# State-space layer with in-place decay matrices, and an order of TensorE's work that is tied to the projections

## The chip, the core and the metric

The kernel runs on one core of a Trainium2 chip. A core has five engines with a queue of instructions each: TensorE (matrix products, PE in the profile, its weight loads PEld), VectorE (DVE), ScalarE (ACT), GpSimd (POOL) and SyncE (SP, which only issues DMAs here). Each engine works through its queue in order and waits on semaphores. The metric is the device time of one execution in microseconds (us); the kernel before was timed three times.

## The reference

The reference is a trunk of two layers over a sequence of 512 tokens of width 1024. Each layer is a half-step SwiGLU feed-forward, a token mixer, and a second half-step feed-forward; every one is modulated, gated, added to the residual and normalised. The mixer of layer 0 is a bidirectional state-space layer, that of layer 1 a differential attention.

```python
for i in range(DEPTH):                      # 2
    y = swiglu(modulate(x, mods[:, 0]), ...)
    x = layer_norm(ALPHA * x + 0.5 * gate(0) * y, ...)
    u = modulate(x, mods[:, 1])
    y = mamba2_bidir(u, ...) if i % 2 == 0 else diff_attention(u, ...)
    x = layer_norm(ALPHA * x + gate(1) * y, ...)
    y = swiglu(modulate(x, mods[:, 2]), ...)
    x = layer_norm(ALPHA * x + 0.5 * gate(2) * y, ...)
```

In the state-space layer, `proj = u @ w_in` gives for each of 4 groups the inputs `xs` (8 heads of 64), `B`, `C` and the gate `z`; `xs`, `B` and `C` go through a convolution of width 3 and a SiLU. Each head then needs, for both directions, `y = (CB * L) X + C states`, where `L` is the matrix of decays, the exponential of differences of cumulated sums. The result is gated by SiLU(z), normalised per group and projected by `w_out`. In the attention, a head takes the difference of two softmaxes, multiplies it with the values, normalises, and the 8 heads are projected by `w_out`.

## The kernel before

Activations lie transposed: 8 tiles of 128 features by 512 tokens (`res`, the residual, and `u`, the input of a stage). Weights come as 128 x 1024 tiles of float32 (`load`, line 93, a DMA by SyncE) and are split into a high part on ScalarE (line 123) and a low part on VectorE (line 124), so that a product of float32 accuracy is three matmuls (`mm3`, line 162; every projection matmul stands on line 166). A projection (`proj`, line 172) of eight 128-blocks and 512 tokens is 24 matmuls of 512 columns.

The program is written as one stream of operations over tiles from rings of buffers (`bufs=`). Before the run a scheduler lays out each engine's queue from that text: an operation that stands earlier has precedence, but a later one is put ahead where the scheduler's own model of the durations says that the earlier one isn't ready. So TensorE's order is not that of the text, and it is fixed once the kernel runs. `tc.add_manual_dep(..., NOSYNC, ...)` ties one instruction behind another in that layout, without a semaphore.

**State-space layer (`ssm`, line 589).** For each group g of 4, in eight half steps (`for s in range(8)`, line 865): at each even s two heads (a pair) are opened by `ssd_head` (line 757). It loads the pair's rows `rw` and `ch` from a scratch in device memory (lines 761 and 763), and GpSimd writes the masks (line 778). For each half c of the sequence, `ssd_mats` (line 783) makes for each head a tile `E` with four exponentials on ScalarE (lines 786 to 789), an addition on GpSimd (line 792) and a multiplication with `cb` on VectorE (line 793); `ssd_out` (line 796) multiplies on TensorE (line 803, `mid` banks). `rw` has a ring of 2 tiles, `E` of 5. Between the half steps stand the projections of the next group (`units_bc`, `units_x`, `units_z`: up to 10) and the output projections of the group before (`outp`, 4 steps). When the projections are done, the SiLUs run in one batch (`silu`, line 711) and `prepare` (line 716) makes the next group's `B` transposed, `cb`, the transposed inputs `xt` and the states: 20 transposes and 8 products on TensorE (lines 721, 729, 742, 751), with copies on ScalarE between them. `gated_norm` (line 805) of the group before stands behind half steps 0 and 2.

**Layer norm (`LN`, line 262).** When the first of the eight residual tiles is complete, `start` (line 269) makes a first guess of the mean and subtracts it from all eight tiles on VectorE (line 278). Each tile that follows gets its addition (`add_res`, line 371, VectorE line 372), then sums and squares (`feed`, line 282). `finish` (line 408) does the last tiles in two halves of the tokens, with `stats` (line 294) and `normalize` behind each.

**End of the attention.** For the last head, h == 7, the output projection of heads 0 to 3 to the first four residual tiles stands between the score steps (`outp`, line 1023). The rest (`merged_units`, line 424) follows behind the last head: heads 4 to 7 to tiles 0 to 3, then all heads to tiles 4 to 7 in halves. The last head's chain is: scores, softmax, transposes (line 987), values (line 998), mean square (line 1004), root (line 247), broadcast (line 253).

## Time and profile before

| | us |
|---|---|
| three timed runs | 2180.67, 2181.95, 2177.81 |
| median | 2180.67 |
| profiled execution | 2176.88 |
| of it the span, first to last instruction | 2174.8 |
| state-space layer, about | 365 to 775 of the span |
| attention, about | 1500 to 1775 of the span |

The page shows busy time of each engine over the span, and the mean granted clock of TensorE is 0.993 of full speed. A stretch in the profile is a window of the span; its row gives the busy time and, in brackets, the number of instructions in it. Where the instructions of one line alone are asked for, the row counts only these. Among the busiest operations beside the matmuls are the weight splits:

```profile
L123 ACT ACTIVATE wh<-raw 128x1024 fp32r<-128x1024 f32 (+1 forms) x210 | 212.8, 1021 | 277.5 <-PE acc L166 95.4
...
L124 DVE TENSOR_TENSOR wl<-raw,wh 128x1024 fp32r<-128x1024 f32 (+1 forms) x210 | 248.4, 1185 | 46.7 <-ACT wh L123 45.4
L471 DVE TENSOR_TENSOR wl<-raw,wh 128x1024 fp32r<-128x1024 f32 x198 | 240.8, 1219 | 38.9 <-ACT wh L470 38.1
```

In such a row stand the line, the engine, what is written and read, the number, then the total busy time in us and the mean of one in ns, then the engine's idle time ahead of them and what ended it.

### The profile page before, as it was taken

Reading aid. Unit: us, or ns where it says so; the run is one execution under the profiler, and the core shown is the slowest. Engines: PE = TensorE matmul, PEld = TensorE weight load, DVE = VectorE, ACT = ScalarE, POOL = GpSimd, SP = SyncE. Lnnn points to the kernel's source line nnn. Section 1 sums busy time; section 2 is a strip of 40 time slices with the busy share of each in tenths; the row PEclk is TensorE's granted clock in tenths of the full one; section 3 lists DMA queues with packets and bytes.
Section 4 is the critical chain, followed back from the end, with each engine's and each line's share of the span. In section 5 each row is a group of like instructions: output and inputs, shape, how many; then the busy total and the mean of one; then the engine's idle time right before and its main releaser. Section 6 shows DMA issues by size and latency. Waiting matters only on the chain.

```text
span 2174.8 us, 34198 instructions
## 1 busy us (share of the span) xinstructions
PE 2119.9 (97%) x13206; PEld 1859.7 (86%) x13206; DVE 1775.3 (82%) x3086; ACT 1092.4 (50%) x1828; POOL 154.2 (7%) x258
## 2 busy tenths in 40 slices
PE   7999999999999989999999999999999989999997
PEld 6889899866777778999999989899888869989897
DVE  6979899556766689989889998987877879858697
ACT  4424354767655546434356534343866637424353
POOL 0000000045232300000000000000111100000000
PEclk9999999999999999999999999999999989999999
DMA  9863644464535423646443273723322212323231
GB/s 324 302 212 121 219 138 149 123 183 137 158 123 155 121 68 126 214 144 198 159 132 105 97 261 96 254 94 111 98 80 79 76 59 78 127 69 117 84 110 39
DMA packets 90082, 301.18 MB, mean 138 GB/s; under 512 B 10048, under 2 KB 13504, under 8 KB 89920
## 3 DMA queue, kind: packets, MB, share of 16 engines
q1 hardware_dynamic: 88384, 294.81, 41.7%
q0 software_dynamic: 1536, 4.20, 0.9%
q8 instruction: 103, 1.69, 0.3%
q14 instruction: 59, 0.48, 0.1%
HBM read 289.53 MB, written 5.24 MB: 136 GB/s over the span
## 4 chain that ended last, share of the span: by engine, by line
PE 59%; DVE 3%; issue 2%; ACT 2%; POOL 1%; DMA 0%; POOLq 0%; ACTq 0%; DVEq 0%; SPq 0%
PE acc L166 47%; PE mid L166 9%; PE mid L965 1%; PE ln L166 1%; PE ln L987 0%; DVE resid L278 0%; DMA raw<-in_wgu 0%; DVE resid L320 0%; PE ln L253 0%; PE ln L302 0%; ACT p L975 0%; POOL E L792 0%; ACT wh L123 0%; PE ln L1004 0%; DVE p L968 0%
## 5 line engine op out<-in xcount | busy, mean ns | idle before, releaser
L166 PE MATMUL acc<-hi,wh 128*128 128x256 f32 (+1 forms) x1592 | 533.1, 336 | 9.2 <-DVE resid L372 7.1
L166 PE MATMUL acc<-hi,wl 128*128 128x256 f32 (+1 forms) x1592 | 532.6, 335 | 0.0
L166 PE MATMUL acc<-lo,wh 128*128 128x256 f32 (+1 forms) x1592 | 532.1, 335 | 0.1
L166 PE MATMUL acc<-uh,wh 128*128 128x256 f32 (+1 forms) x1160 | 391.2, 338 | 0.0
L166 PE MATMUL acc<-ul,wh 128*128 128x256 f32 (+1 forms) x1160 | 389.6, 336 | 0.0
L166 PE MATMUL acc<-uh,wl 128*128 128x256 f32 (+1 forms) x1160 | 388.9, 336 | 0.0
L123 ACT ACTIVATE wh<-raw 128x1024 fp32r<-128x1024 f32 (+1 forms) x210 | 212.8, 1021 | 277.5 <-PE acc L166 95.4
L166 PEld LDWEIGHTS acc<-hi,wh 128*128 128x128 f32 x1592 | 302.9, 190 | 45.5 <-DVE resid L372 6.6
L470 ACT ACTIVATE wh<-raw 128x1024 fp32r<-128x1024 f32 x198 | 209.1, 1059 | 259.4 <-DVE raw L480 129.1
L166 PEld LDWEIGHTS acc<-lo,wh 128*128 128x128 f32 x1592 | 302.9, 190 | 31.0 <-DVE lo L154 1.3
L166 PEld LDWEIGHTS acc<-hi,wl 128*128 128x128 f32 x1592 | 303.0, 190 | 30.3 <-issue 0.5
L124 DVE TENSOR_TENSOR wl<-raw,wh 128x1024 fp32r<-128x1024 f32 (+1 forms) x210 | 248.4, 1185 | 46.7 <-ACT wh L123 45.4
L471 DVE TENSOR_TENSOR wl<-raw,wh 128x1024 fp32r<-128x1024 f32 x198 | 240.8, 1219 | 38.9 <-ACT wh L470 38.1
L166 PEld LDWEIGHTS acc<-uh,wh 128*128 128x128 f32 x1160 | 219.0, 189 | 28.6 <-issue 6.2
L166 PEld LDWEIGHTS acc<-ul,wh 128*128 128x128 f32 x1160 | 219.3, 189 | 25.1 <-issue 3.2
L166 PEld LDWEIGHTS acc<-uh,wl 128*128 128x128 f32 x1160 | 219.2, 189 | 23.7 <-issue 2.4
L480 DVE TENSOR_TENSOR raw<-raw 128x512 f32<-128x512 f32 x264 | 181.3, 688 | 5.0
L184 DVE SCALAR_TENSOR_TENSOR raw<-raw,cond 128x1024 f32<-128x1024 f32 x144 | 174.1, 1218 | 9.9 <-DMA raw<-in_adaw 9.7
L372 DVE SCALAR_TENSOR_TENSOR resid<-acc,gv,resid 128x512 f32<-128x512 f32 (+1 forms) x166 | 109.4, 663 | 58.8 <-PE acc L166 58.4
L316 POOL TENSOR_TENSOR rr<-vr,mhalf 128x2 f32<-128x2 f32 x12 | 8.4, 698 | 1527.6 <-DVE vr L312 1527.6
L166 PE MATMUL mid<-uh,wh 128*128 128x256 f32 (+2 forms) x332 | 99.8, 302 | 0.0
L166 PE MATMUL mid<-uh,wl 128*128 128x256 f32 (+2 forms) x332 | 99.3, 299 | 0.0
(266 smaller groups left out, 3920.7 us busy)
## 6 DMA issues: line engine op xcount, KB each, us to landing
raw<-in_wgu SPq DMA_DIRECT2D x176, 512.0 KB, 4.2
raw<-in_adaw SPq DMA_DIRECT2D x144, 512.0 KB, 4.6
raw<-in_wdn SPq DMA_DIRECT2D x64, 448.0 KB, 4.0
raw<-in_win SPq DMA_DIRECT2D x40, 512.0 KB, 4.2
raw<-in_wdn SPq DMA_DIRECT2D x32, 512.0 KB, 4.4
rw<-scr SPq DMA_DIRECT2D x32, 512.0 KB, 5.5
ch<-scr SPq DMA_DIRECT2D x32, 256.0 KB, 3.6
raw<-in_wso SPq DMA_DIRECT2D x16, 512.0 KB, 3.5
```

The costliest lines, as they stand in the source:

```text
L123: nc.scalar.activation(hi[:, :n], raw, AF.Copy)
L124: nc.vector.tensor_tensor(out=lo[:, :n], in0=raw, in1=hi[:, :n].bitcast(F32), op=ALU.subtract)
L166: last = nc.tensor.matmul(o, lhsT=a, rhs=b, start=start and j == 0, stop=j == n - 1, skip_group_check=not start)
L184: nc.vector.scalar_tensor_tensor(out=raw, in0=raw, scalar=1.0, in1=cond, op0=ALU.mult, op1=ALU.mult, accum_out=mods[l][:, j : j + 1],)
L316: nc.gpsimd.tensor_tensor(out=r[:, :m], in0=vr[:, :m], in1=mhalf[:, :m], op=ALU.pow)
L372: nc.vector.scalar_tensor_tensor(out=res[d][:, a:b], in0=pd[:, a:b], scalar=gvec[n][:, d : d + 1], in1=res[d][:, a:b], op0=ALU.mult, op1=A ...
L470: nc.scalar.activation(x[0], r, AF.Copy)
L471: nc.vector.tensor_tensor(out=x[1], in0=r, in1=x[0].bitcast(F32), op=ALU.subtract)
L480: nc.vector.tensor_tensor(out=o, in0=x, in1=y, op=ALU.add)
L965: nc.tensor.matmul(ss[m], lhsT=q[:, c], rhs=qks[h, 1][m], start=j == 0, stop=j == 1)
```

## The change

It has four parts.

1. **Matrices in place.** The exponentials are written over the rows `rw`; the tile `E` and its ring go. The ring of `rw` has 6 tiles instead of 2, and `fetch` loads the rows of the next pair at the start of a pair; the first pair's are loaded ahead of the first SiLUs.
2. **Order in the state-space layer.** A group has four steps, one for each pair, instead of eight half steps. A pair's masks and exponentials come first, then its share of the projections, then the product of both halves. `gated` ties an instruction of TensorE behind the last matmul of the last projection (`shut` notes it): so each pair's products stand behind all of that step's projections, a group's preparation behind the first projection of the group (it was at the end of the group before), and the two parts of the norm behind the second projection and the first one of the next pair.
3. **Layer norm.** The first guess of the mean is subtracted from each tile when that tile is fed, not from all eight at once.
4. **End of the attention.** The output projection of heads 0 to 3 to tiles 0 to 3 stands behind the last score steps; half products of the same heads for tiles 4 and 5 are begun in `mid` banks between the last head's values, mean square and broadcast, and are completed later (`begun` in `finish`). The last head's steps are tied behind these pieces.

```diff
-NE = 5
+NRW = 6
...
+    def gated(x):
+        if gate[0] is not None:
+            tc.add_manual_dep(x.ins, gate[0].ins.name, NOSYNC, reason="behind a projection")
+        return x
+
+    def shut():
+        gate[0] = last_mm[0]
...
-            for d in range(KT):
-                nc.vector.tensor_tensor(out=res[d], in0=res[d], in1=m0, op=ALU.subtract)
+            self.near = set()
...
+            if d not in self.near:
+                self.near.add(d)
+                nc.vector.tensor_tensor(out=res[d], in0=res[d], in1=self.m0, op=ALU.subtract)
...
-                pd = acc()
-                proj(pd, w, u, cols=((a, b),))
+                if a == 0 and d in begun:
+                    pd, k0 = begun[d]
+                    last_mm[0] = mm3(pd[:, a:b], [(*w[k], *(x[:, a:b] for x in u[k])) for k in range(k0, len(u))], start=False)
+                else:
+                    pd = acc()
+                    proj(pd, w, u, cols=((a, b),))
...
+        for q in range(2):
+            w = split(load(wo[q]))
+            for e in range(2):
+                pd, d = acc(), 2 * q + e
+                proj(pd, w[e * 4 : e * 4 + 4], old)
+                add_res(d, pd, n, 0, T)
+                yield
+        w0 = {2: split(load(wo[2]), home=home[0])}
+        begun = {}
+        for e in range(2):
+            pd = acc("mid")
+            proj(pd, w0[2][e * 4 : e * 4 + 4], old, cols=HALVES[:1])
+            begun[4 + e] = (pd, half)
+            yield
...
+        def fetch(ft):
+            if ft >= 16:
+                return
+            for h in (2 * ft, 2 * ft + 1):
+                rw = ep.tile([P, 2, T], F32, tag="rw", name="rw", bufs=NRW)
+                nc.sync.dma_start(rw, scr[:, h].unsqueeze(1)[:, :, 0:2].broadcast_to([16, 8, 2, T]))
+                rows_of[h] = rw
...
+            i, cc = 2 * c, slice(c * W, (c + 1) * W)
+            nc.scalar.activation(rw[:, 0, cc], rw[:, 0, cc], AF.Exp, bias=bias[:, i, h : h + 1])
+            nc.scalar.activation(rw[:, 1, cc], rw[:, 1, cc], AF.Exp, bias=bias[:, i + 1, 32 + h : 33 + h])
...
+            for pr_ in range(4):
                 ft = g * 4 + pr_
...
+                fetch(ft + 1)
+                heads = [ssd_head(ft * 2 + hh, Ct) for hh in range(2)]
+                for c in range(2):
+                    for hh in range(2):
+                        ssd_mats(ft * 2 + hh, c, heads[hh][0], heads[hh][2])
+                if pr_ == 0:
+                    step()
+                    if cur is None:
+                        shut()
+                        cur = prepare(g, *coming)
+                    xt, cbs, states, Ct = cur
+                    cur = None
+                for c in range(2):
+                    for hh in range(2):
+                        ssd_mul(c, heads[hh][0], cbs)
+                if pr_ == 0 and norm is not None:
+                    step()
+                    shut()
                     rest = norm()
...
+                if pr_ == 1 and norm is not None:
+                    step()
+                    shut()
                     yrs[g - 1] = rest()
...
+                while done < (pr_ + 1) * tot // 4 - (2 if g == NG - 1 and pr_ == 3 else 0):
+                    step()
+                shut()
+                py = acc("mid")
+                ssd_out(pr_, heads, py, xt, states)
+                gate[0] = None
...
+        for f in back[:-3]:
             f()
...
+        fill(3)
+        back[-3]()
+        fill(1)
+        back[-2]()
+        back[-1]()
+        gate[0] = None
+        next(end)
+        send(end, [os_[h] for h in range(4, 8)])
```

In the last part `fill(k)` takes the next k pieces of `merged_units` and then calls `shut`; `values` calls it once ahead of the mean square and once ahead of the broadcast.

More of the change, by code (lines that the diff above doesn't have):

```diff
@@ L104, in hybrid_trunk, with split @@
     first_ln = [None]
-    turn, period = [0], [2]
-    def split(raw, where=None):
+    turn = [0]
+    def split(raw, where=None, home=None):
         n = raw.shape[-1]
@@ L422, in finish, with merged_units @@
         ln.residual()
-    def merged_units(n, old, wo, new, wn, full=4):
+    def merged_units(n, old, wo, wn, home):
         ln = LN(n)
-        for q in range(full // 2):
+        half = len(old)
+        for q in range(2):
[12 more added lines that the diff above has]
+            yield
+        new = yield
+        for q in range(2):
             w = split(load(wn[q]))
@@ L434, in merged_units, with send @@
         keep = []
-        for q in range(full // 2, 4):
-            w0, w1 = split(load(wo[q])), split(load(wn[q]))
+        for q in range(2, 4):
+            w1 = split(load(wn[q]), home=home[q - 1])
+            if q == 3:
+                w0[3] = split(load(wo[3]), home=home[3])
             for e in range(2):
                 c = slice(e * 4, e * 4 + 4)
-                keep.append((2 * q + e, w0[c] + w1[c], old + new))
-        finish(n, ln, keep)
+                keep.append((2 * q + e, w0[q][c] + w1[c], old + new))
+        finish(n, ln, keep, begun)
+    def send(g, x):
+        try:
+            g.send(x)
+        except StopIteration:
+            pass
     def input_forms(u):
@@ L844, in ssm @@
         run(units_x(0, xs)[2:])
+        fetch(0)
         silu(bc + xs)
@@ L862, in ssm @@
                 first = units_bc(g + 1, nbc) + units_x(g + 1, nxs) + first
[L863 to L877 removed]
+            late = lambda gg, k: [lambda: outp(gg)] * k
@@ L1020, in attention @@
         os_ = {}
-        og = []
-        def outp():
-            if not og:
-                og.append(down_units(n, [os_[h] for h in range(4)], wide_units(wao[0]), False))
-            next(og[0])
         back, rests = [], []
```

139 lines of the change are left out of this document (69 added, 70 removed).

## The prediction

> **What bounds the kernel now.** I read the page first, then who waited for whom (total us, times, longest), then stretches (bounds and length; busy us and instructions of TensorE's matmuls, its weight loads, VectorE, ScalarE and GpSimd; granted clock, DMA share, GB/s), then instructions in order of time.
>
> ```profile
> PE 2119.9 (97%) x13206; PEld 1859.7 (86%) x13206; DVE 1775.3 (82%) x3086; ACT 1092.4 (50%) x1828; POOL 154.2 (7%) x258
> ```
> ```profile
> PE acc L166 <- DVE resid L372: 7.1, 3, 4.4
> PE mid L803 <- DVE E L793: 4.7, 3, 3.6
> ```
> ```profile
> 461.00:509.50 48.50, 43.83 (x194) 28.23 (x193) 31.20 (x41) 30.44 (x72) 21.77 (x40) 0.96 0.76 205
> 1776.40:1796.00 19.60, 15.17 (x104) 14.87 (x102) 16.39 (x32) 4.36 (x9) 0.00 (x0) 0.83 0.25 77
> ```
>
> TensorE is the bound: busy 97% of the span. Busy time does not say how much work there was. In the stretch 461 to 509.5 it is busy 43.83 of 48.50 us, and the work in it is much less, as a count shows. The prices of that count are in TensorE's order of time (start, duration, number; in brackets an idle time and what ended it):
>
> ```profile
> 443.17 0.40 PE L166 MATMUL acc<-uh,wh 128*128 128x512 f32 x1
> ...
> 457.94 0.39 PE L166 MATMUL acc<-uh,wl 128*128 128x512 f32 x1
> ...
> 461.00 0.50 PE L166 MATMUL acc<-uh,wh 128*128 128x512 f32 x1
> ...
> 561.04 1.08 PE L803 MATMUL mid<-E,xt 128*64 128x256 f32 x8
> ...
> 568.17 1.08 PE L803 MATMUL mid<-E,xt 128*64 128x256 f32 x8
> ```
> ```profile
> 1764.47 1.05 PE L1004 MATMUL ln<-inve,sq 128*128 128x1 f32 x8 [0.69 <-ACT sq L1000]
> 1766.93 0.65 PE L253 MATMUL ln<-csts,rr 128*128 128x128 f32 x4 [1.41 <-POOL rr L247]
> 1769.16 2.07 PE L166 MATMUL acc<-hi,wh 128*128 128x512 f32 x4 [1.57 <-ACT hi L153]
> 1771.03 0.63 PE L166 MATMUL acc<-lo,wh 128*128 128x512 f32 x1
> ```
>
> **Prices.** One projection matmul (512 columns): 65 steps from one start to the next lie between 443.17 and 457.94, so 0.227 us each, although each is 0.39 us long; that is why busy overstates. A whole pair's product, both halves in one block (24 instructions of L803): from 457.94 + 0.227 to 461.00 = 2.83 us; I take 3.0, allowing for the restart behind it. A half product alone (12 instructions): the cycle 561.04 to 568.17 is 7.13 us and holds 24 projection matmuls (5.45), so 1.68. Two halves cost 3.36, a joined pair 3.0. A gated norm adds 8 narrow matmuls and 4 transposes; by the rows at 1764.47 and 1766.93 (same shapes) and their overlap I charge 1.4. The counts, for projections (L166) and then pair products (L803), each with matmuls and weight loads of that line alone (a count can hold one that straddles an edge):
>
> ```profile
> 415.20:442.30 27.10, 21.13 (x84) 15.48 (x85) 1.00 0.91 197
> 461.00:509.50 48.50, 31.34 (x120) 22.01 (x120) 0.96 0.76 205
> 509.50:548.50 39.00, 26.02 (x97) 17.43 (x96) 1.00 0.36 105
> 593.20:616.30 23.10, 13.23 (x49) 8.72 (x48) 1.00 0.44 132
> 616.30:694.60 78.30, 67.34 (x289) 53.51 (x288) 1.00 0.47 140
> 694.60:717.10 22.50, 13.31 (x49) 8.72 (x48) 1.00 0.41 123
> 717.10:762.80 45.70, 34.41 (x145) 26.57 (x144) 1.00 0.46 133
> 762.80:774.50 11.70, 4.50 (x18) 3.09 (x18) 0.99 0.40 135
> ```
> ```profile
> 461.00:509.50 48.50, 13.98 (x74) 6.08 (x72) 0.96 0.76 205
> 509.50:548.50 39.00, 5.65 (x38) 2.34 (x38) 1.00 0.36 105
> 593.20:616.30 23.10, 2.15 (x12) 0.95 (x12) 1.00 0.44 132
> 616.30:694.60 78.30, 10.61 (x84) 5.41 (x84) 1.00 0.47 140
> 694.60:717.10 22.50, 2.18 (x14) 0.97 (x14) 1.00 0.41 123
> 717.10:762.80 45.70, 9.71 (x72) 4.79 (x72) 1.00 0.46 133
> ```
>
> **The change, part by part.**
>
> **Group 0's pairs (461 to 509.5).** 120 projections at 0.227 are 27.2; the other 21.3 us went to three pairs, worth 9.0. So 12.3 us are lost. The cause is seen on GpSimd and on TensorE: the masks wait for the decay rows, and a product that was queued too early holds TensorE, for 3.6 us at the longest (L803 waiting for L793, in the waits above). In the order of time, and then by line (minimum, median and maximum in ns):
>
> ```profile
> 475.55 0.77 POOL L778 TENSOR_SCALAR_AFFINE_SELECT rw<-rw 128x256 f32<-128x256 f32 x2 [8.98 <-DMA rw<-scr]
> ```
> ```profile
> 444.81 0.51 ACT L786 ACTIVATE E<-rw,ssbias 128x256 f32<-128x256 f32 x1
> ```
> ```profile
> 447.60 0.76 ACT L678 ACTIVATE xc<-acc,pars 128x512 f32<-128x512 f32 x1
> ```
> ```profile
> L792 POOL TENSOR_TENSOR E<-E,dx x64: 720/740/1708, 446.4 to 761.4; 128x256 f32<-128x256 f32 x64
> ```
> ```profile
> L793 DVE TENSOR_TENSOR E<-E,cb x64: 675/691/1249, 447.2 to 762.7; 128x512 f32<-128x512 f32 x64
> ```
>
> The ring of rows grows from two tiles to six and the next pair's rows are fetched a pair ahead, so the 8.98 us wait should go. What is late next is the chain behind the rows: per pair 8 masks (0.77 for two, 3.1), 16 exponentials (two sets of four from 444.81 to 447.60, so 5.6 for four sets), 4 adds (0.74 each), 4 multiplies (0.69 each). They overlap in a pipe; the longest member is 5.6, and with a first mask set, a last add and a last multiply it is about 8.5. The cover is the two projections tied ahead of each product, 2 x 24 x 0.227 = 10.9 us. It holds by 2.4; without it a product would wait up to 8.5. Bounds: 4.7 (the idle part, 48.50 - 43.83) and 12.3; I take 12.3, since the 8.98 us wait that starts the loss goes whole.
>
> **Preparation of groups 1 to 3.** Group 0's stands between projections alone: 27.1 - 84 x 0.227 = 8.0 us. The others are woven with half products. 509.5: 39.0 - 22.0 - 1.4 - 1.5 pairs (4.5) = 11.1. 593.2: 23.1 - 11.1 - 1.5 = 10.5. 694.6: 22.5 - 11.1 - 1.5 = 9.9. At 8.0 each this gains 3.1 + 2.5 + 1.9 = 7.5. The step moves from the end of one group to behind the first projection of the next. With it go its nine copies on ScalarE, now behind the first pair's 16 exponentials (5.6 us), and four multiplies on VectorE; the first pair's four multiplies then wait for its copies. What hides this is the first projection (5.45 us) ahead and two or more behind; without it TensorE stands for those 5.6 us, in each of three groups. Bounds: -16.8 by that, to 11, should a third of 8.0 be waits that go too. I take 7.5, group 0 being the nearest row.
>
> **Joined halves in groups 1 to 3.** 616.3: 78.3 - 65.6 - 1.4 = 11.3 for 3.5 pairs, worth 10.5: 0.8. 717.1: 45.7 - 32.9 - 1.4 = 11.4 for 3 pairs, worth 9.0: 2.4. Together 3.2 (bounds 0, should the parts not join, and 3.2). The last stretch, 11.7 - 4.1 - 3.0 - 1.4 = 3.2 us lost, is the last group's norm, which the change leaves ungated: nothing counted.
>
> **In-place matrices.** The multiply, add and exponentials keep count and size: nothing. The tile is now held until TensorE has read it, and the fetch waits for that in SyncE's queue, with weight loads behind it. Six tiles are three pairs: the fetch of pair p+1 waits for the product of p-2, over a pair earlier. The first pair's two fetches move ahead of the SiLUs and of two weight loads, which three split weight tiles cover. Cost 0; with that cover gone, one projection, 5.5 us.
>
> **Waits added.** A gated product stands at the head of TensorE's in-order queue, and all projections behind it wait with it; so do the bank evacuations on VectorE and ScalarE that free the next weights. Bounds for one product: 0 to the longest seen, 3.6. I take 0.1 for each of 16: 1.5 in all (near 0, by the cover of 10.9).
>
> **End of attention.** Two half products (24 matmuls of 256 columns, an estimate of half of 0.227 each, 2.7 us) leave the stretch 1776.4 to 1796 and go where TensorE waits 0.69 and 1.41 (rows 1764.47, 1766.93); the 0.6 that doesn't fit delays the chain to the last head. The four full projections of the old heads and their weight loads move behind the last head's scores in the text, but nothing ties them from above, and the order may place them as early as now: 0. The eight subtractions become one ahead of the first addition and one ahead of each later one:
>
> ```profile
> 1776.49 4.90 DVE L278 TENSOR_TENSOR resid<-resid,m 128x512 f32<-128x512 f32 x8
> 1781.30 1.41 DVE L372 SCALAR_TENSOR_TENSOR resid<-acc,gv,resid 128x512 f32<-128x512 f32 x2
> ```
>
> The addition at 1781.30 can start 7/8 of 4.90 = 4.3 us earlier, and TensorE's longest wait for it (4.4) nearly goes. But VectorE does the same work in all and is busy 16.39 of the 19.60 us there, so at most 3.2 come out: VectorE is late next. With the delay taken off that is 2.6. The clock adds something (granted 0.83 in 1776.4 to 1796): from 1769.16 to 1771.03 four matmuls start 0.47 apart instead of 0.227, after TensorE had waited 0.69, 1.41 and 1.57. Twelve such matmuls at 0.2 extra are 2.4 us; with two of three gaps filled I take 1, bounds 0 and 2.4. The Trainium skill ("TensorE: Matmul & The Clock Gate", section "Why this matters for your kernels") lets the clock fall only after idle gaps of about 3 us or more; no gap here was longer than 1.57, so by the page there is no slow clock to win back and the sum is 1 us less, but the spacing of 0.47 disagrees, and the trace decides. Sum for this part 3.5, bounds -0.6 and 8.
>
> **Subtractions in the other norms.** The three waits sum to 7.1, so the other two have 2.7. The work on VectorE is unchanged; I take 0.5, bounds 0 and 2.7.
>
> **Sum:** 12.3 + 7.5 + 3.2 - 1.5 + 3.5 + 0.5 = 25.5 us, so 26. Against the profiled execution (2176.88 us, of which 2174.8 are the span) this is 2151; the median of the three timed runs, 2180.67, lies 3.8 above, and the forecast is set on it: 2180.67 - 26 = 2154.7, so **2154 us**. Those runs spread over 0.19%, about what can be told from no change.
>
> **Rivals.**
>
> **The gates make TensorE wait (slower).** Every product now waits for its whole pair, with nothing behind able to pass. For it: the 3.6 us of one such wait now, and the third pair product of the last group has the fourth right behind it. Against it: 10.9 us or more of cover elsewhere. It decides from 27 / 16 = 1.7 us a product; at 3.6 each, 58 - 27 gives 2180.67 + 31 = 2212. Chance 6%.
>
> **Only idle time comes back.** Ties from one side leave preparation woven, and only the row fetch helps: the 7.5 go, and of group 0's 12.3 half of what is not idle (7.6 / 2 = 3.8). 26 - 7.5 - 3.8 = 14.7 gives 2166. For it: the busy share, if it is read as work. The Trainium skill ("Perfetto Trace Analysis", "Identifying the Most-Contended Engine") advises against that reading and takes weight-load time; here that is 28.23 of 48.50 us, 58%, against 86% over the span, which agrees with the count. Chance 22%.
>
> **The tails and the waits go as well.** No new waits (1.5), the last norm's 3.2, attention's upper bound (4.5 more), the other norms (2.2): 11.4 more, 2143. Chance 13%.
>
> **It does not do what it says.** The ties are laid on an order that is made before the run; it may come out as now, with rows as late as now. 2180. Chance 5%.
>
> **Chances and range.** Forecast 54%. Faster 0.54 + 0.22 + 0.13 = 0.89, same 0.05, slower 0.06. The range runs from the third rival with 3 us for preparation's upper bound, 2140, to the second with 4 more should the joined halves bring nothing, 2170; outside lie the slower case, no change, and edges of the others, under 2 in 10.
>
> **What would show it.** Right: L803's instructions in 16 runs of 24, without a projection between; masks no longer waiting for rows after the first pairs; the slow-clock stretches gone from 461 to 509; preparation at about 8 us beside its projections; additions into the residual not behind eight subtractions. Wrong: TensorE waiting for the multiplies (L793's successor) over 1.7 us a product, weight loads waiting in SyncE behind row fetches, or projections still woven through preparation with the 10 us it has now.

## The result, and the profile after

The changed kernel is slower. Its four timed runs have a median of 2196.13 us (2194.53 to 2198.37), the kernel before 2180.81 us on the same chip (2177.81 to 2181.95): 15.3 us less. The ratio on record is 1.0078, 95% interval 1.0066 to 1.0090, which is some 17 us; the experiments below are compared by this ratio. The forecast was 2154 us and its range ended at 2170. Time went the other way.

The page after, total busy times:

```profile
PE 2123.4 (97%) x13206; PEld 1865.1 (85%) x13206; DVE 1780.2 (81%) x3086; ACT 1090.3 (50%) x1826; POOL 167.9 (8%) x258
```

TensorE's instructions are the same in number (13206) and still 97% busy. Nothing in this line says where 17 us went. The stretch from the first pair product to the last group's norm sums does; first the kernel before, then after (bounds and length; busy us and instructions of matmuls, weight loads, VectorE, ScalarE, GpSimd; granted clock, DMA share, GB/s):

```profile
458.20:771.60 313.40, 301.79 (x1455) 216.84 (x1455) 209.76 (x280) 194.66 (x392) 107.05 (x175) 0.99 0.49 142
```
```profile
460.60:792.20 331.60, 302.34 (x1468) 223.65 (x1468) 214.34 (x282) 190.00 (x381) 114.86 (x169) 0.97 0.47 136
```

18.2 us more in this stretch, of the 21.8 us between the two profiled spans (2174.8 and 2196.6; the profiled executions lie 3.9 us below and 2.2 us above their medians). The second row holds 13 matmuls more (x1468 against x1455), output projections that came earlier, 3.0 us at the prediction's 0.227, so the stretch lost some 15.2 us. It starts 2.4 us later as well; in two experiments whose code is that of the change up to there it starts at 458.3 (e7) and 461.5 (e14), so this much is the spread of one profiled execution. Inside the stretch, the place that was to give most, group 0's pairs, with the same instructions of TensorE as in the prediction's row for 461.00 to 509.50 (48.50 us, x194, clock 0.96):

```profile
463.40:518.70 55.30, 42.42 (x194) 29.77 (x192) 32.30 (x40) 32.97 (x76) 32.10 (x43) 0.88 0.61 171
```

6.8 us longer for the same 194 matmuls, while busy time fell from 43.83 to 42.42: TensorE stood, and the clock sagged to 0.88. And the preparations of groups 1 to 3, projections alone, then pair products alone (matmuls, weight loads, clock, DMA share, GB/s):

```profile
518.60:544.30 25.70, 13.60 (x49) 8.73 (x48) 1.00 0.43 124
622.80:645.10 22.30, 13.65 (x49) 8.80 (x48) 1.00 0.27 77
724.20:749.50 25.30, 11.61 (x35) 6.65 (x33) 0.93 0.23 69
```
```profile
724.20:749.50 25.30, 3.79 (x24) 1.82 (x24) 0.93 0.23 69
```

By the prediction's count: 25.7 - 48 x 0.227 (10.9) = 14.8; 22.3 - 10.9 = 11.4; 25.3 - 34 x 0.227 (7.7) - one pair (3.0) = 14.6. Together 40.8 us, against 11.1 + 10.5 + 9.9 = 31.5 before and 24.0 forecast. So 6.8 + 9.3 = 16.1 us, slightly more than the 15.2 of the whole stretch, were lost in two places which were to gain 12.3 and 7.5.

Who waited for whom after, between 440 and 800 us (us in all, times, longest):

```profile
PE ln L794 <- DVE xd L790: 6.8, 5, 2.1
PE mid L857 <- DVE rw L846: 5.9, 2, 4.6
PE acc L176 <- ACT wh L123: 4.3, 1, 4.3
PE mid L857 <- DVE ch L815: 3.4, 1, 3.4
PE acc L176 <- DVE wl L124: 2.6, 1, 2.6
PE ln L772 <- ACT bt L766: 2.1, 1, 2.1
```

The lines after: L176 projections, L857 pair products (before L803), L123 and L124 the two copies that split a weight tile, L836 to L839 the exponentials, L846 the multiplies (before L793), L807 the fetch of rows, L814 that of a ch tile and L815 its multiply, L829 the masks on GpSimd, L766, L777 and L787 the preparation's copies on ScalarE, L790 its multiplies on VectorE, L99 the load of a weight tile. Two kinds of wait are new in the list: projections that wait for their own split weights (L123, L124), and a preparation that waits for its copies (0.2 us in all before). The waits for xd and bt above, one for cb (2.0 us) and one for xc (1.5 us) all lie in the preparations: 12.4 us there, against 3.6 before (xd 3.4, xt 0.2). So 8.8 of the 9.3 us that the preparations lost are such waits. The longest for xd, 2.1 us, is in group 3; VectorE there:

```profile
731.26 4.70 DVE L846 TENSOR_TENSOR rw<-rw,cb 128x512 f32<-128x512 f32 x5
735.88 1.21 DVE L790 TENSOR_TENSOR xd<-xt,dd 128x512 f32<-128x512 f32 x1
```

The copy that this second multiply reads was done at 733.6 us. VectorE was busy until 735.9 with five multiplies of the first pair's matrices, which stand ahead of it.

**Where group 0 stands.** Pairs are counted from 0. TensorE in order of time, after (start, duration, number; in brackets the idle time before it and what ended it):

```profile
462.88 0.60 PE L857 MATMUL mid<-ch,st 128*64 128x256 f32 x4
468.10 2.14 PE L857 MATMUL mid<-rw,xt 128*64 128x256 f32 x7 [4.62 <-DVE rw L846]
...
478.71 0.65 PE L176 MATMUL acc<-uh,wh 128*128 128x512 f32 x1 [4.35 <-ACT wh L123]
...
488.31 0.63 PE L176 MATMUL acc<-ul,wh 128*128 128x512 f32 x1
488.74 0.58 PE L176 MATMUL acc<-uh,wl 128*128 128x512 f32 x1
```

Pair 1's product follows pair 0's with nothing between, waits, and then there is no projection to run: the weights aren't split. ScalarE's splits after:

```profile
443.18 1.05 ACT L123 ACTIVATE wh<-raw 128x1024 fp32r<-128x1024 f32 x1
...
473.46 0.51 ACT L836 ACTIVATE rw<-rw,ssbias 128x256 f32<-128x256 f32 x1 [9.36 <-POOL dx L829]
...
477.62 1.99 ACT L123 ACTIVATE wh<-raw 128x1024 fp32r<-128x1024 f32 x2
```

and before:

```profile
451.70 2.06 ACT L123 ACTIVATE wh<-raw 128x1024 fp32r<-128x1024 f32 x2
458.14 1.06 ACT L123 ACTIVATE wh<-raw 128x1024 fp32r<-128x1024 f32 x1 [4.37 <-PE acc L166]
468.61 1.06 ACT L123 ACTIVATE wh<-raw 128x1024 fp32r<-128x1024 f32 x1 [2.55 <-DMA raw<-in_win]
```

For 34.4 us, from 443.18 to 477.62, no weight tile is split; the kernel before splits four between 451.70 and 468.61. ScalarE was not short of time: it stood 9.36 us for pair 2's masks, with the splits behind those exponentials. And the loads themselves were late, by SyncE's queue (issues in order of time):

```profile
443.15 0.36 SPq L99 DMA_DIRECT2D raw<-in_win  x1
463.50 0.52 SPq L814 DMA_DIRECT2D ch<-scr  x1
464.11 1.19 SPq L807 DMA_DIRECT2D rw<-scr  x2
...
466.00 2.97 SPq L99 DMA_DIRECT2D raw<-in_win  x3
```

20.0 us without an issue: the second ch tile of pair 1 needs a buffer of a ring of three, which the whole product of pair 0 frees, and two rows, a ch tile and three weight loads stand behind it. The two rows are those of pair 3, and on GpSimd their masks stand ahead of the last masks of pair 2, for which ScalarE waits:

```profile
470.62 0.77 POOL L829 TENSOR_SCALAR_AFFINE_SELECT rw<-rw 128x256 f32<-128x256 f32 x2 [8.97 <-DMA rw<-scr]
```

The trace thus has the chain whole: product of pair 0, ch tile, rows of pair 3, masks, exponentials of pair 2, splits, projections. It is also the wait of 8.98 us for rows that the prediction said would go whole; it is there again, at 8.97.

### The profile page after: what moved, and what is told of

Read it like the earlier page. It is cut to its first block, busy times and chain, and to the rows that moved or that the text cites. A ratio compares the mean times of both kernels' runs of the same rounds, so it can differ in the third digit from the quotient of the medians.

```text
span 2196.6 us, 34174 instructions
## 1 busy us (share of the span) xinstructions
PE 2123.4 (97%) x13206; PEld 1865.1 (85%) x13206; DVE 1780.2 (81%) x3086; ACT 1090.3 (50%) x1826; POOL 167.9 (8%) x258
## 4 chain that ended last, share of the span: by engine, by line
PE 81%; DVE 9%; DMA 4%; ACT 3%; issue 2%; POOL 1%; SPq 0%; POOLq 0%; ACTq 0%; DVEq 0%
PE acc L176 65%; PE mid L176 9%; PE mid L857 2%; DMA rw<-scr 2%; DMA raw<-in_adaw 1%; PE mid L1044 1%; DVE raw L195 1%; DVE wl L124 1%; PE ln L176 1%; DMA ch<-scr 1%; DVE resid L334 1%; DVE wl L513 1%; DVE raw L522 1%; PE ln L794 1%; PE ln L1066 0%
## 5 line engine op out<-in xcount | busy, mean ns | idle before, releaser
L176 PE MATMUL acc<-hi,wh 128*128 128x256 f32 (+1 forms) x1576 | 525.8, 335 | 2.5 <-DVE resid L386 1.8
L176 PE MATMUL acc<-hi,wl 128*128 128x256 f32 (+1 forms) x1576 | 525.2, 334 | 0.7 <-DVE wl L124 0.7
L176 PE MATMUL acc<-lo,wh 128*128 128x256 f32 (+1 forms) x1576 | 524.8, 334 | 0.4 <-DVE lo L154 0.4
L176 PE MATMUL acc<-uh,wh 128*128 128x256 f32 (+1 forms) x1160 | 392.6, 339 | 4.5 <-ACT wh L123 4.3
L176 PE MATMUL acc<-ul,wh 128*128 128x256 f32 (+1 forms) x1160 | 392.6, 338 | 0.7 <-DVE ul L1162 0.7
L176 PE MATMUL acc<-uh,wl 128*128 128x256 f32 (+1 forms) x1160 | 390.6, 337 | 2.6 <-DVE wl L124 2.6
L123 ACT ACTIVATE wh<-raw 128x1024 fp32r<-128x1024 f32 (+1 forms) x210 | 212.9, 1021 | 270.3 <-DMA raw<-in_wdn 102.2
L176 PEld LDWEIGHTS acc<-hi,wh 128*128 128x128 f32 x1576 | 297.8, 189 | 36.6 <-ACT hi L153 3.8
L176 PEld LDWEIGHTS acc<-lo,wh 128*128 128x128 f32 x1576 | 298.3, 189 | 31.8 <-DVE lo L154 2.1
L176 PEld LDWEIGHTS acc<-hi,wl 128*128 128x128 f32 x1576 | 298.1, 189 | 30.5 <-DVE wl L124 0.9
L124 DVE TENSOR_TENSOR wl<-raw,wh 128x1024 fp32r<-128x1024 f32 (+1 forms) x210 | 247.5, 1182 | 54.0 <-ACT wh L123 52.5
L176 PEld LDWEIGHTS acc<-uh,wh 128*128 128x128 f32 x1160 | 220.0, 190 | 32.3 <-ACT wh L123 5.7
L176 PEld LDWEIGHTS acc<-uh,wl 128*128 128x128 f32 x1160 | 220.0, 190 | 26.8 <-DVE wl L124 3.3
L176 PEld LDWEIGHTS acc<-ul,wh 128*128 128x128 f32 x1160 | 220.2, 190 | 24.1 <-issue 1.4
L176 PE MATMUL mid<-uh,wh 128*128 128x256 f32 (+2 forms) x332 | 100.2, 303 | 0.6 <-DVE up L554 0.6
L176 PE MATMUL mid<-ul,wh 128*128 128x256 f32 (+2 forms) x332 | 99.5, 300 | 0.0
```

The costliest lines, as they stand in the source:

```text
L123: nc.scalar.activation(hi[:, :n], raw, AF.Copy)
L124: nc.vector.tensor_tensor(out=lo[:, :n], in0=raw, in1=hi[:, :n].bitcast(F32), op=ALU.subtract)
L176: last = nc.tensor.matmul(o, lhsT=a, rhs=b, start=start and j == 0, stop=j == n - 1, skip_group_check=not start)
```

## Experiments

Each kernel is timed against the kernel before on its own chip, so the ratios are what is compared (us: median of the timed runs):

| kernel | us | ratio to before | 95% interval |
|---|---|---|---|
| the change | 2196.13 | 1.0078 | 1.0066 to 1.0090 |
| e1: a fourth ch tile | 2190.14 | 1.0051 | 1.0038 to 1.0063 |
| e2: no ties | 2194.30 | 1.0070 | 1.0056 to 1.0084 |
| e3: preparation at the end of the group | 2196.92 | 1.0078 | 1.0064 to 1.0092 |
| e4: state-space stage of before | 2181.79 | 1.0011 | 1.0002 to 1.0019 |
| e5: matrices of their own, rows not ahead | 2192.41 | 1.0047 | 1.0029 to 1.0066 |
| e6: rows not ahead | 2200.04 | 1.0090 | 1.0075 to 1.0105 |
| e7: evacuations tied to half a pair | 2195.29 | 1.0071 | 1.0055 to 1.0086 |
| e8: rows on GpSimd's queue | 2195.37 | 1.0072 | 1.0057 to 1.0087 |
| e9: e1, exponentials in eights | 2195.61 | 1.0072 | 1.0057 to 1.0087 |
| e10: e1, weights loaded and split ahead | 2178.30 | 0.9993 | 0.9984 to 1.0003 |
| e11: e10, exponentials tied behind splits | 2181.05 | 1.0006 | 0.9996 to 1.0015 |
| e12: e9 and e3 | 2195.43 | 1.0071 | 1.0056 to 1.0086 |
| e13: e1, weights only loaded ahead | 2183.73 | 1.0022 | 1.0011 to 1.0032 |
| e14: e10, no ties | 2177.15 | 0.9993 | 0.9984 to 1.0003 |
| e15: e10 and e3 | 2176.49 | 0.9987 | 0.9977 to 0.9996 |
| e16: e15, exponentials behind the copies | 2176.39 | 0.9983 | 0.9973 to 0.9993 |
| e17: e16's stage without ties, rest as before | 2178.73 | 1.0000 | 0.9990 to 1.0011 |
| e18: e17, norm one pair later | 2185.58 | 1.0031 | 1.0019 to 1.0043 |

### Which part holds the loss: e4

The state-space stage of the kernel before is put into the changed kernel (the whole function).

> The state-space stage is the one of the kernel before; what stays of the change is the end of attention and the subtractions ahead of each addition. If the whole loss is in the state-space stage (theories A, B and C alike, some 19 us of it between 415 and 795 us in the traces), the time is 2178 to 2183 us. If the 2.4 us that the changed kernel has lost before 361 us come from the subtractions, 2183. If the end of attention gives what was forecast (3.5 and 0.5 for the other norms), 2177; the traces speak for no gain: 7.7 us won by 1824 us and all of it given back by 1841 us.

2181.79 us, 0.1% over before: all but some 2 us of the loss is in the state-space stage. By the ratios the stage costs 1.0078 - 1.0011 = 0.67%, 14.6 us, which fits the 15.2 of the two rows. The rest of the change, the end of attention and the deferred subtractions, gives nothing; whether it costs the 2 us is taken up with e17.

### The ring of ch: e1

```diff
-            ch = ep.tile([P, T], F32, tag="ch", name="ch", bufs=3)
+            ch = ep.tile([P, T], F32, tag="ch", name="ch", bufs=4)
```

> Theory A (the ring of the ch tiles): in the changed kernel SyncE's queue stands 20.0 us at 443 to 463 us for the second ch tile of pair 1, whose buffer is freed only by the first pair's whole product, with the rows of pair 2 and the weight loads behind it; that makes pair 1's product wait 4.9 us and the projections behind it lose 11.2 us. With a fourth ch tile (nothing else changed) the 20 us go and the time falls by 10 to 16 us, to 2180 to 2186 us. Theory B (the preparation behind the first pair's exponentials on ScalarE is what costs): at most 3 us come back, 2193 to 2196. Theory C (the ties make TensorE wait, whatever the rows do): the same as theory B here.

1.0051: 0.27% or 6 us came back, half of what theory A wanted, and not where it wanted it. SyncE's queue of e1:

```profile
462.62 1.16 SPq L807 DMA_DIRECT2D rw<-scr  x2
...
465.11 1.62 SPq L99 DMA_DIRECT2D raw<-in_win  x3
```

Both ch tiles of pair 1 are issued by 441.6 us now, and the next issue stands 21.0 us all the same: the rows of pair 3, whose tile the product of pair 0 frees, since the matrices are made in it. (The rows behind the 20 us are pair 3's too, not pair 2's as the expectation has it.) Group 0 hardly gains (the rows stand with e10 below). The gain is in the last group. From the sums of group 2's norm to those of group 3's, the change and then e1:

```profile
750.20:792.20 42.00, 38.16 (x197) 27.99 (x197) 28.48 (x41) 18.63 (x34) 8.28 (x13) 0.96 0.42 120
```
```profile
747.08:780.86 33.78, 32.39 (x183) 24.40 (x182) 26.35 (x39) 19.14 (x34) 7.96 (x13) 1.00 0.49 141
```

8.2 us less, of which the 14 matmuls that now lie elsewhere are 3.2 and the rest 5.0; the product's wait for its ch tile (L815, 3.4 us) is gone.

### The ties: e2, e7 and e14

e2 takes every tie on TensorE away:

```diff
     def gated(x):
-        if gate[0] is not None:
-            tc.add_manual_dep(x.ins, gate[0].ins.name, NOSYNC, reason="behind a projection")
         return x
```

> All ties of the order on TensorE are taken away, every other part of the change stays. Theory C (the ties make TensorE wait): the time falls by 10 us or more, to 2186 or less. Theory A: SyncE's wait for the ch tile stays, since the ring is as small; the time stays within 4 us of 2196. Theory B: the preparation still stands behind the first pair's exponentials in the text; within 4 us of 2196 as well.

1.0070, an interval that overlaps that of the change: the ties are not the cause. TensorE's order came out nearly the same without them; pair 1's product still waits 4.7 us for its multiply.

e7 shrinks a tie that was there before, which now spans sixteen exponentials:

```diff
-            last_exp[0] = e if h < 24 else None
+            if c == 0:
+                last_exp[0] = e if h < 24 else None
```

> One line: the bank evacuations of the projections are tied behind the last exponential of a pair's first half, as before, and no longer of the whole pair. Theory D: the evacuations and the weight splits come up to 2.8 us (eight exponentials) earlier behind each pair; 5 us or more back, 2192 or less. Theory A2 and E: within 3 us of 2197.

1.0071: nothing. Theory D falls. e14 takes the ties away once the weights are there (e10):

> As e10 with all ties on TensorE taken away. If the ties give what the change wants of them once the weights are there: slower than e10 by 3 us or more, 2181 or more. If they do nothing or hold TensorE up: 2173 to 2179.

0.9993 both with and without, and in the state-space stage the matmuls stand in the same order in both traces: the ties bought nothing, with the weights there or without.

### Rows: e5, e6 and e8

e6 fetches a pair's rows at its own start. e5 does so too and gives the exponentials tiles of their own again (a ring of eight; the ring of rows goes back to two), so that ScalarE frees the rows.

```diff
-                fetch(ft + 1)
+                fetch(ft)
...
-            nc.scalar.activation(rw[:, 0, cc], rw[:, 0, cc], AF.Exp, bias=bias[:, i, h : h + 1])
+            E = ep.tile([P, T], F32, tag="E", name="E", bufs=8)
+            nc.scalar.activation(E[:, :W], rw[:, 0, cc], AF.Exp, bias=bias[:, i, h : h + 1])
```

> In place as changed, six row tiles, but each pair's rows are fetched at its own start and not a pair ahead. Theory A2: the fetch stands one pair later in SyncE's queue, more weight loads are ahead of it; 3 to 8 us back, 2189 to 2194. If the fetch ahead is worth what was forecast for group 0, this is slower than 2197 instead. Theories D and E: within 3 us of 2197.

> The exponentials write matrices of their own again (a ring of eight tiles) and the rows have their ring of two, fetched at the pair's start; joined pairs, ties, the later preparation and the rest stay as changed. Theory A2 (in place, a row tile is freed only by TensorE's product, and its fetch stands in SyncE's queue ahead of the weight loads; with four ch tiles the 20 us wait only moved on to the rows of the fourth pair, 21.0 us): the rows are freed by ScalarE, so 8 to 14 us of the 17 come back, 2183 to 2189 us. Theory D (a tie that was there before, the bank evacuations of the projections behind the last exponential in the text, now spans 16 exponentials instead of 8): no more than 3 us, 2194 to 2197. Theory E (joined pairs with one-sided ties as such): the same as D.

e6: 1.0090, some 3 us slower than the change with intervals that overlap, so the fetch ahead is not the harm, and the 3 to 8 us that theory A2 wanted back here did not come. e5: 1.0047, 0.31% or 7 us back from the change (the intervals touch at 1.0066), a little under what theory A2 wanted (8 to 14), and 0.43% or 9 us from e6, from which it differs only in the tiles: holding a row tile until TensorE has read it is a part of the loss. It is not all of it.

e8 moves the rows and ch tiles to GpSimd's queue (`nc.gpsimd.dma_start` in place of `nc.sync.dma_start` in both).

> The rows and the ch tiles are fetched from GpSimd's queue, so no weight load stands behind them in SyncE's; all else as changed. Theory A2: the waits of SyncE before weight loads behind rows go, and with them 8 us or more: 2189 or less, if GpSimd's own masks are not held up more than that. Theory D and E: no gain; with the fetches in GpSimd's order ahead of masks, 2197 or slower.

1.0072: no gain. Who waited in e8, SyncE's queue between 436 and 515 us:

```profile
SPq L99 <- DVE wl L124: 96.2, 9, 34.2
```

With no row in the queue, a weight load still waits 34.2 us, now for a free raw tile, that is for a split that has not been made (L124 is its second half). The splits stand in ScalarE's queue behind exponentials, so theory A2 alone can't hold. The run is no clean test of it, though: the fetches of rows now wait in GpSimd's queue, 57.2 us in all for products over the whole span, and GpSimd's masks stand behind them. The Trainium skill ("Trainium Kernel Development and Optimization", section "Key Constraints") says that transfers issued from SyncE, ScalarE and GpSimd share the same 16 engines, and that issuing from several saves issue time only. e8's time agrees; but in the changed kernel's trace an issue that waits for a buffer also keeps 20.0 us of later ones back, which the sentence doesn't speak of.

### The splits behind the exponentials: e9 to e13

e10 loads and splits the weights of a pair's first two projections in the text ahead of its rows and exponentials:

```diff
+        ready_w = {}
+        def weight(k):
+            return ready_w.pop(k) if k in ready_w else split(load(win[k]))
+        def ahead(units):
+            for f in units:
+                if hasattr(f, "k") and f.k not in ready_w:
+                    ready_w[f.k] = split(load(win[f.k]))
...
             for pr_ in range(4):
                 ft = g * 4 + pr_
+                ahead(todo[done : done + 2])
                 fetch(ft + 1)
```

e13 does the same with `load` alone and leaves the split where it was; both have four ch tiles.

> Four ch tiles, and the weights of a pair's first two projections are loaded and split in the text ahead of the pair's rows and its sixteen exponentials, so that neither SyncE's weight loads nor ScalarE's splits stand behind them. Theory F, and A2 for the loads: 4 to 12 us less than 2190, 2178 to 2186. If neither queue is what starves TensorE in group 0, 2188 to 2192.

> As e10, but only the loads of the two next weight tiles stand ahead of the pair's rows; the copies that split them stand behind the sixteen exponentials in the text, as in the change. Theory F (the splits behind the exponentials in ScalarE's queue starve TensorE): as with four ch tiles alone, 2188 to 2192, and no weight tile is split between 443 and 470 us. Theory A2 (the loads behind the rows in SyncE's queue): as e10, 2176 to 2181.

e10 gives 0.9993, 0.58% or 13 us under e1. e13 lies halfway, 1.0022, and the intervals of e1, e13 and e10 don't touch: about 6 us come from the loads in SyncE's queue and 6 from the splits in ScalarE's. Neither theory had it alone. No run loads and splits ahead in the kernel before, so it stays open how much of these 13 us that kernel would gain as well; that they reach the place of the loss is seen in group 0. Here it is from its first product to the preparation of group 1, the same 217 matmuls each time; before, the change, e1, e13 and e10 in that order:

```profile
458.20:509.50 51.30, 46.62 (x217) 29.87 (x217) 31.20 (x41) 33.24 (x78) 22.11 (x40) 0.97 0.72 194
```
```profile
460.60:518.70 58.10, 45.22 (x217) 31.40 (x216) 32.30 (x40) 35.77 (x82) 33.08 (x46) 0.88 0.58 163
```
```profile
460.15:517.35 57.20, 45.72 (x217) 31.38 (x217) 37.10 (x45) 38.21 (x87) 33.25 (x46) 0.88 0.67 190
```
```profile
461.00:514.10 53.10, 43.83 (x217) 31.47 (x216) 35.38 (x43) 36.86 (x85) 31.26 (x46) 0.90 0.65 178
```
```profile
459.35:504.85 45.50, 41.42 (x217) 30.92 (x216) 34.40 (x42) 35.53 (x81) 32.18 (x45) 0.96 0.74 205
```

The lengths, 51.30, 58.10, 57.20, 53.10 and 45.50, tell it in one column. GpSimd's wait for the rows of pair 3, 8.97 us in the change and 8.93 in e1, is 4.99 in e10. The first split after the pause shows why, in e13 and in e10 (477.62 in the change, 477.81 in e1):

```profile
468.51 2.00 ACT L123 ACTIVATE wh<-raw 128x1024 fp32r<-128x1024 f32 x2
```
```profile
461.34 2.00 ACT L123 ACTIVATE wh<-raw 128x1024 fp32r<-128x1024 f32 x2
```

e9 tries it another way: four ch tiles, and a pair's exponentials in two sets of eight with a projection between.

```diff
-                for c in range(2):
-                    for hh in range(2):
-                        ssd_mats(ft * 2 + hh, c, heads[hh][0], heads[hh][2])
-                if pr_ == 0:
-                    step()
+                for hh in range(2):
+                    ssd_mats(ft * 2 + hh, 0, heads[hh][0], heads[hh][2])
+                step()
+                for hh in range(2):
+                    ssd_mats(ft * 2 + hh, 1, heads[hh][0], heads[hh][2])
+                if pr_ == 0:
```

> Four ch tiles, and each pair's exponentials are in the text in two sets of eight with a projection between, as before the change, instead of sixteen ahead of it; in place, fetched ahead, joined, tied and with the later preparation as changed. Theory F (sixteen exponentials of a pair, which wait for rows and masks, stand in ScalarE's in-order queue ahead of the copies that split the weights: from 443.2 to 477.6 us the changed kernel splits no weight tile, the kernel before has four between 451.7 and 468.6, and TensorE has nothing to multiply): against four ch tiles alone (2190) 4 to 10 us less, 2180 to 2186. Theory A2 (SyncE's queue behind a row tile that only a product frees): no change from 2190.

A miss: 1.0072, 5 us more than e1. Group 0 did gain (50.70 us for 218 matmuls, from 57.20), but the last group lost it: its output projections wait for the normed values' split on ScalarE, once and for 5.8 us (L176 for hi, L153).

e11 is e10 with the exponentials tied behind the last split:

> As e10, and the exponentials are tied behind the last split in the text, so that ScalarE's order can't be otherwise. Theory F: as e10 or up to 4 us better. The other way: the exponentials come so late that products wait, 2190 or more.

1.0006, 3 us over e10, with intervals that overlap: the order in the text was enough. TensorE's waits for xd grow from 7.4 to 9.5 us with the tie and those for bt fall from 6.3 to 2.6; whether the tie costs anything is not shown.

### The preparation: e3, e12, e15 and e16

e3, e12 and e15 put it back to the end of the group before, in the change, in e9 and in e10:

```diff
             coming = (nxs, nbc)
+            if g < NG - 1:
+                cur = prepare(g + 1, nxs, nbc)
```

> The preparation of groups 1 to 3 goes back to the end of the group before, behind its last product; all else as changed. By the count of the two traces it costs 14.7, 11.4 and 15.0 us in the changed kernel (without its projections and products) and 11.1, 10.5 and 9.9 before. Theory B: these 9.6 us come back, 2186 us, and the waits of TensorE for xd, bt and cb shrink to those of the kernel before. Theory A or C: less than 3 us, 2193 to 2196.

> As e9, and the preparation goes back to the end of the group before. Theory B2 (the later place costs when ScalarE's sets are of eight as before; alone, among sets of sixteen, moving it back gave nothing): against e9 another 3 to 8 us less, since its nine copies are then ahead of the first pair's exponentials. If the place of the preparation is worth nothing either way: within 3 us of e9.

> As e10 with the preparation of groups 1 to 3 at the end of the group before. In e10 it costs 16.4, 12.0 and about 12 us beside its projections, against 11.1, 10.5 and 9.9 in the kernel before and 8.0 in group 0. Theory B2 (the later place costs): 4 to 9 us less than e10, 2169 to 2174. If the place in the text does nothing, since the first pair's exponentials are ready early and go ahead on ScalarE either way: within 3 us of e10.

1.0078 after 1.0078, 1.0071 after 1.0072, 0.9987 after 0.9993: the place in the text is worth nothing that can be told from no change, so theories B and B2 fall in the form in which they were put. What is ahead of the copies on ScalarE is another question, and e16 asks it: e15 with the next group's exponentials tied behind the last copy (L787).

> As e15, and the exponentials of the next group are tied behind the last of the preparation's copies on ScalarE. If the copies behind exponentials are what makes the preparation dear: its cost falls toward 8.0 us in each of three groups, 4 to 12 us less than e10, 2166 to 2174. The other way: the first product of each group now waits for exponentials that start late, 2178 or more.

0.9983, within 1 us of e15: less than expected. But the waits show that the mechanism is there. TensorE's waits between 440 and 800 us in e15:

```profile
PE ln L802 <- ACT xt L804: 5.2, 2, 2.6
...
PE ln L811 <- DVE xd L807: 2.8, 4, 1.4
```

and in e16:

```profile
PE ln L893 <- DVE gss L890: 7.1, 4, 3.1
...
PE ln L812 <- DVE xd L808: 2.2, 2, 1.8
```

The waits for the copies are gone (xt, 5.2 us in e15; in e10 it was bt, 6.3). Those for xd had already fallen from 7.4 in e10 to 2.8 in e15 and are 2.2 here. The sums of the gated norm, which come next on the same two engines, are late in their place (7.1, in e15 no such wait, in e10 1.7). What the preparation wins in this order, the norm loses.

### What is left: e17 and e18

e17 is e16's stage without ties in the kernel before. e18 calls the gated norm one pair later:

```diff
-                if pr_ == 0 and norm is not None:
-                    step()
+                if pr_ == 1 and norm is not None:
                     rest = norm()
-                if pr_ == 1 and norm is not None:
-                    step()
+                if pr_ == 2 and norm is not None:
                     yrs[g - 1] = rest()
```

> The state-space stage of e16 without ties, in the kernel before: the end of attention and the subtractions are those of before. The other way round (the stage of before in the changed kernel) cost 0.1% against before. If the rest of the change costs those 2 us wherever it stands, 2174 to 2175, 0.2 to 0.3% faster than before; if it costs nothing, 2176 to 2178.

> As e17, with the gated norm of the group before one pair later: in e16 TensorE waits 3.2 and 2.1 us for the sums of that norm in groups 1 and 2, since the preparation now stands ahead of it on VectorE and ScalarE. If those waits go and nothing takes their place: 4 to 7 us less than e17, 2168 to 2171. If the output projections that need the norm are late instead: no faster than e17.

e17: 1.0000, no better than e16, so the 2 us of e4 are not shown to be a cost of the rest of the change. e18: 1.0031, 7 us worse: the waits for the sums grow from 6.7 to 10.8 us. The lowest ratio is e16's, 0.17% under the kernel before (0.07 to 0.27%), which is at the edge of what can be told.

## Why the prediction was wrong

The two large terms had the wrong sign, and both fell at the step that named their cover. One of the prediction's own signs of being wrong came: weight loads waiting in SyncE's queue behind row fetches.

| term | forecast gain, us | measured, us |
|---|---|---|
| group 0's pairs | 12.3 | -6.8 |
| preparation of groups 1 to 3 | 7.5 | -9.3 |
| joined halves | 3.2 | 2.5 |
| in-place matrices | 0 | inside the -6.8 |
| waits added | -1.5 | -9.3, of it 5.9 inside the -6.8 |
| end of attention | 3.5 | -0.4 |
| other norms | 0.5 | not seen alone |

**"In-place matrices ... Cost 0."** This is the step that failed first. The prediction saw that the fetch waits in SyncE's queue with weight loads behind it, and dismissed it twice: by the ring of six ("over a pair earlier") and by three split weight tiles as cover. The six tiles were counted against the products in the text; in the order that was made, the rows of pair 3 stand in SyncE's queue ahead of the weights for the projections behind pair 0's product, and their tile is the one that pair 0's product frees, so the queue waits for that product (20.0 us by ch, 21.0 by rows in e1). The ring of the ch tiles, three for two pairs, was not looked at at all. Three split tiles are three projections, 3 x 5.45 = 16.4 us, and the pause in the splits was 34.4. The price "with that cover gone, one projection, 5.5 us" was too small as well: the loads ahead gave 6 us, and the fourth ch tile another 6, most of them in the last group.

**"The cover is the two projections tied ahead of each product, 10.9 us. It holds by 2.4."** The tie is from one side. Group 0's projections ran as early as their weights allowed, ahead of pair 0's product, as they did before; so pair 1's product came right behind it and waited 4.62 us, and then the projections had no weights. A tie that says "not before" provides no cover; only weights that are split in time do. Nor did the prediction ask where the splits stand: it put the sixteen exponentials (5.6 us) on ScalarE as a member of the products' chain, not as what stands ahead of the weights' chain in the same queue. The splits ahead gave the other 6 us of e10. With loads, splits and a fourth ch tile in place, group 0 takes 45.50 us in e10 against 51.30 before: 5.8 of the 12.3 us that were forecast.

**Preparation at 8.0.** The bound of -16.8 had named half of the mechanism: nine copies behind sixteen exponentials. It was set aside for "group 0 being the nearest row"; but group 0's preparation has no exponentials beside it, so it was the wrong neighbour. The measured -9.3 lies between the ends of -16.8 and 11, nearer to the one that was dropped from the range. (The 11 is a slip: a third of 8.0 in each of three groups is 8.0, and 7.5 + 8.0 = 15.5. And 7.5 - 16.8 happens to be -9.3, but the trace has 12.4 us of waits there, not 16.8: that is luck.) Of the 12.4 us, 5.6 wait for ScalarE (xc, bt, cb) and 6.8 for xd. Ahead of two of the waits for xd, of 1.59 and 2.12 us, stand five of the first pair's multiplies on VectorE, 4.70 us in each case. The prediction asked how the pair's multiplies wait for the copies, and not how the preparation's own multiplies wait for the pair's. e3 shows that moving the step back doesn't undo it, e16 that putting the copies first does, at the price of the norm. Why the preparation is dearer after than before even with the place undone (e3: 5.3 us for xd, 5.0 for xc and 4.0 for xt) is only argued here: a pair's sixteen exponentials and eight multiplies come in one set, early, since the rows are there.

**Joined halves** were right in kind and size. The stretch after the third group's preparation, projections and products:

```profile
645.00:724.25 79.25, 66.82 (x289) 53.67 (x288) 1.00 0.52 151
```
```profile
645.00:724.25 79.25, 11.88 (x96) 6.71 (x96) 1.00 0.52 151
```

79.25 - 288 x 0.227 (65.4) - 1.4 = 12.4 for four pairs, 3.1 each (forecast 3.0). The 6.5 pairs that took 11.3 + 11.4 = 22.7 us before would take 20.2: 2.5. What is left of the stage, 15.2 - 16.1 + 2.5 = 1.6 us, lies in the rest of it; the last group, where a product waits 3.4 us for its ch tile and e1 won 5.0 back, is a part of that.

**End of attention.** "VectorE is late next" was right and was then costed too mildly. From the first projection of the new heads to the same place in the FFN (some 2365 matmuls from the end in both) it takes 48.70 us before and 49.10 after. Before, then after, in two parts:

```profile
1769.10:1808.40 39.30, 34.79 (x231) 33.10 (x232) 32.79 (x72) 18.11 (x34) 0.70 (x1) 0.85 0.19 56
1808.40:1817.80 9.40, 8.99 (x70) 8.45 (x70) 8.40 (x28) 8.46 (x17) 0.72 (x1) 1.00 0.12 49
```
```profile
1792.20:1823.80 31.60, 29.04 (x198) 26.30 (x198) 30.68 (x70) 18.84 (x34) 0.70 (x1) 0.95 0.21 68
1823.80:1841.30 17.50, 15.05 (x69) 13.31 (x69) 14.70 (x38) 12.22 (x25) 0.69 (x1) 0.61 0.17 53
```

7.7 us are won up to the second half's statistics (39.30 to 31.60). 33 of the 231 matmuls of the first row, narrow ones of 256 columns, now lie ahead of it, in the waits of the last head's chain, 4.0 us at the 0.12 that such a matmul takes below. VectorE is busy 30.68 of those 31.60 us. Behind this, TensorE is ahead of the normalised values that the FFN needs, waits for them, and 8.1 us go back (9.40 to 17.50). The wait for the additions, which the prediction showed at 4.4 us, did go; VectorE's work did not.

**The rivals.** The slower one, "the gates make TensorE wait", has the right sign and the wrong cause: without gates the time is the same (e2), and the waits of products came to 5.9 + 3.4 = 9.3 us, 0.6 each, not 1.7. "Only idle time comes back" and "the tails and the waits go as well" forecast a gain, and "it does not do what it says" no change. The range left out both of the bounds that the text itself had worked out for covers that fail: -16.8 for the preparation and -5.5 for the fetch.

## What to carry to other kernels

A buffer that is freed later is paid in the queue of whatever refills it: list what stands behind that transfer, and behind each exponential that now runs earlier, before calling the cost nothing. A tie that says "not before" is no cover; in a kernel that TensorE bounds, put the loads and splits of the next weights ahead of any work that may wait. A bound worked out from a cover that could be gone belongs in the range.

## What the runs showed of the hardware

TensorE's clock fell in two places. In group 0 the matmuls from 484 to 488.74 us start 0.43 us apart, not 0.227, after waits of 4.62 and 4.35 us; that agrees with the Trainium skill ("TensorE: Matmul & The Clock Gate", section "Why this matters for your kernels"), which warns of idle gaps of more than about 3 us. At the start of the FFN no gap was as long:

```profile
1821.05 0.58 PE L176 MATMUL acc<-ul,wah 128*128 128x256 f32 x1 [0.69 <-DVE ul L364]
...
1834.61 0.41 PE L176 MATMUL acc<-ul,wah 128*128 128x256 f32 x1
1834.82 0.41 PE L176 MATMUL acc<-uh,wal 128*128 128x256 f32 x1
```

Between 1806 and 1821.05 us the longest idle time is 0.69 us, in a row of 0.60, 0.45 and 0.69 from 1817.1 us on; the longest behind it are 0.92 and 1.40. Yet the matmuls from 1821 us on are at 0.21 us a step (1834.61 to 1834.82) where the same shape takes 0.12 at 1815 us, and the granted clock is 0.61 in the second of the two stretches shown for the end of attention, 0.95 in the first. So gaps of that length are not the only way to a slow clock here; which property of these short waits brings it is not shown.
